# Two hybrid layers on one core: pieces of wide products inside the triangular solves, and a block transpose for a third merge

## The chip, the core and the metric

The kernel runs on one NeuronCore of a Trainium2 chip. Its engines work side by side, each through its own instructions in order: TensorE (PE, matrix products into PSUM), VectorE (DVE, elementwise work, reductions and transposes of 32x32 blocks), ScalarE (ACT, activations and copies), GpSimd (POOL, here memsets, gathers and the issue of some DMAs) and SyncE (SP, issues DMAs). An engine waits at an instruction until what it needs is there, and everything behind it on that engine waits too.

The metric is the device time of one execution in microseconds (us). Before the change it was 4466.47 us, the median of three runs (4464.66 to 4471.57).

## The reference

Two layers work on 256 latent tokens and 256 context tokens of width 1024. Cut to what matters here, a layer is

```python
h = adaLN(RMSNorm(x))
z = h @ w_in                      # r, k, v, decay and rate inputs, conv inputs, gates
# RWKV-7, 16 heads of 64, both directions; per head and token t
S = S * w_t - (S @ kk_t) (kk_t * a_t)^T + v_t k_t^T
y_t = S @ r_t
y_a = (groupnorm(y) + bonus) * sigmoid(g1) @ g2 @ w_oA
y_b = silu(layernorm(depthwise_conv31(u * sigmoid(u2)))) @ w_oB
x += gate1 * ((sigmoid(gA) * y_a + sigmoid(gB) * y_b) @ w_out)
x += gate2 * PEER(adaLN(RMSNorm(x)))   # top-16 of 16384 experts, 8 heads
```

In the last layer the context tokens only feed the recurrent state, so most products there have 256 columns instead of 512. A last RMSNorm gives the output. The change touches only the part called the mixer, from `z` to the inputs of `w_oA`.

## The kernel before

**Chunks and solves.** The recurrence is worked in chunks of 64 tokens. Within a chunk, the tokens' mutual influence is a unit triangular matrix of 64x64 that has to be inverted. The 16 heads go in 8 pairs, one head on the upper and one on the lower 64 partitions. For a pair j, `front(j)` makes what the chunks need: the decay and rate products (`lora`, tile `up`), the key norm (`rnc`, `rnb`), the scaled keys (`KR`, `BK`), then `solve`. `solve` forms the triangular matrices of all 16 (chunk, direction) pairs at once (`pd`, L689, and the off-diagonal blocks `po`, L705). It inverts the 16x16 diagonal blocks on DVE by a recurrence of 15 steps (`Tn`, L715 and L717), then joins blocks by matrix products on PE. A *merge* is 64 matmuls of 32x32 with 32 columns. Three merges (L735, tile `m`) make the inverse of the 32x32 blocks: the first multiplies by `Dg` and is masked into `PA`; the second gives `T32`, the inverse; the third gives `Td`, the transposed inverse, from the transposed factors. Two half merges of 32 matmuls each (L755 and L767, called fourth and fifth here) make the last off-diagonal block. Fp32 matmuls are recorded twice, so a merge has 128 records.

**Chains and wide products.** `chain(j)` then walks through the 8 chunks of pair j with products of 64x64 (tile `p`; `wp` and `tr` beside it), each step waiting for copies on ACT and DVE. `tail(j)` normalises the pair's output. The *wide products* are the columns of `w_in`: `project(j)` makes k, r and v of a pair (24 products), `conv(j)` two products per group of conv channels, `gate(i)` one for each of 16 groups of gates, `lora_g(i)` two. Each is done by `dense_w`: 24 matmuls of 128x128 (tile `dn`, lines L350 to L352) with 512 or 256 columns, three for each of 8 pieces of the weights, which are split into a high and a low part (`whi`, cast on ACT, L132; `wlo`, subtracted on DVE, L133). There are two buffers for each of raw, high and low weights. `conv_sum(j)` does the depthwise convolution on DVE, and `conv_ln`, `yb` (tile `dn` from `chi`) and `gg` (tile `gp`) finish the mixer behind the last pair.

**What sets the order.** Each of these is a Python generator, registered by `job` with a start, an end and a number of steps. The loop at the end of the mixer (L985) always takes one step of the live job whose due time is earliest; times are counted in pairs of heads. A job's first step first runs those it needs to their end. All of `project(2..7)`, `conv`, `gate` and `lora_g` stand in one line (`order`, L949 to L971), each needing the one before it, spread evenly over 0 to `DENSE` = 7.5, and a piece of it is three matmuls. The steps that `solve` yields are weighed (`W_MRG`, `W_SMALL`, `W_TRI`). The compiler's scheduler then places instructions of each engine by priority in about that order, and gives buffers from what is free.

Of the kernel before, what the change touches and what calls it, by code (L numbers as in the profile page):

```python
# [88 lines left out]
def body(ctx: ExitStack, tc: tile.TileContext, I, out):  # L89
# [125 lines left out]
    for l in range(2):  # L215
# [74 lines left out]
        with tc.tile_pool(name="psR", bufs=1, space=PSUM) as pr, tc.tile_pool(name="rw", bufs=1) as rw:  # L290
# [381 lines left out]
            def solve(KR, BK, TT, extra):  # L672
# [11 lines left out]
                for d in range(2):  # L684
                    for c in range(8):
                        for b in range(2):
                            for hh, hs in enumerate(heads):
                                q, cs = hh * 64 + 32 * b, slice(32 * b, 32 * b + 32)
                                mm(pd[q:q + 32, d * 8 + c], BK[d][hs, c // 2, 1 + c % 2, cs], KR[d][hs, c, 0, cs],  # L689
                                   start=True, stop=True)  # L690
                        if c % 2 == 1:
                            yield 0.25
# [9 lines left out]
                for d in range(2):  # L702
                    for c in range(8):
                        for hh, hs in enumerate(heads):
                            mm(po_[lo_[hh], d * 8 + c], BK[d][hs, c // 2, 1 + c % 2, 0:32], KR[d][hs, c, 0, 32:64],  # L705
                               start=True, stop=True)
                        if c % 4 == 3:
                            yield 0.25
# [23 lines left out]
                def merge(pq, lhs, rhs):  # L732
                    for u in range(16):
                        for q in quads:
                            mm(pq[q, u], lhs[q, u], rhs[q, u], start=True, stop=True)  # L735
                        if u % MU == MU - 1:
                            yield W_MRG * MU
# [10 lines left out]
                pq = pt("m3")  # L748
                yield from merge(pq, PA, T16t)
                dve.tensor_tensor(Td, pq, T16t, op=OP.add)  # L750
                yield W_SMALL
                pq = pt("m4")
                for u in range(16):
                    for hh in range(2):
                        mm(pq[hi_[hh], u], Of[lo_[hh], u], T32[lo_[hh], u], start=True, stop=True)  # L755
                    if u % MU == MU - 1:
                        yield W_MRG * MU / 2
# [7 lines left out]
                for u in range(16):  # L765
                    for hh in range(2):
                        mm(pq[lo_[hh], u], PB[hi_[hh], u], Td[hi_[hh], u], start=True, stop=True)  # L767
                    if u % MU == MU - 1:
                        yield W_MRG * MU / 2
# [157 lines left out]
            def step(i):  # L927
                t0, t1, n, gen, needs, k = jobs[i]
                for d in needs if k == 0 else ():
                    while jobs[d][3] is not None:  # L930
                        step(d)
                w = next(gen, jobs)
                if w is jobs:
# [3 lines left out]

            def due(i):
# [3 lines left out]
            NF = 4 * W_LORA + 2 * W_RMS + 15 * W_TRI + 15 * W_VEC + 12 * W_SMALL + 32 * W_MRG * 2 + 3.2  # L942
# [5 lines left out]
            job(conv_sum(0), 0, 0.5, 19, cv0)  # L948
            order = []  # L949
            for j in range(2, 8):  # L950
                order += [("p", j), ("c", j - 1)] + [("g", None)] * (1 if j < 7 else 0)
            order += [("c", 7)] + [("g", None)] * 11 + [("z", 0), ("z", 1)]
            njobs = sum({"p": 3, "c": 2, "g": 1, "z": 1}[a] for a, _ in order)
            t, gi, prev = 0.0, 0, None
            for a, j in order:
                if a == "p":
                    g, n = project(j), 3
                elif a == "c":
                    g, n = conv(j), 2
                elif a == "g":  # L960
                    g, n = gate(gi), 1
                    gi += 1
                else:
                    g, n = lora_g(j), 1
                t1 = t + n * DENSE / njobs
                prev = job(g, t, t1, 8 * n, *([] if prev is None else [prev]))
                if a == "p":
                    pj[j] = prev
                elif a == "c":
                    lastc = job(conv_sum(j), t1, t1 + 0.5, 19, prev)  # L970
                t = t1  # L971
# [540 lines left out]
```

## Time and profile before

| | before |
|---|---|
| median of 3 runs | 4466.47 us |
| profiled execution | 4484.19 us, span of instructions 4482.4 us |
| PE busy | 4079.7 us (91%) |
| DVE busy | 3190.2 us (71%) |
| ACT busy | 2108.8 us (47%) |
| POOL busy | 275.1 us (6%) |
| mean granted clock of TensorE | 0.927 |
| mixer of layer 0 | about 60 to 988 us |
| mixer of layer 1 | about 2640 to 3440 us |

The span runs from the first to the last instruction. Busy PE is not PE at its best: a matmul counts as busy from its start to a modelled end, and at the lower of the two clock levels (1.2 instead of 2.4 GHz) it simply takes longer. The clock granted is a mean over the stretch asked for, where 1.00 is the full level and 0.50 the lower one.

### The profile page before, as it was taken

What the parts mean: (1) busy time and instruction counts of PE and PEld (TensorE: products, weight loads), DVE (VectorE), ACT (ScalarE), POOL (GpSimd) and SP (SyncE); (2) the same over time, 40 slices, a digit from 0 to 9 for tenths busy, and PEclk for the clock granted to TensorE, in tenths of its full rate; (3) what the DMA queues carried; (4) which work ended last, traced back from release to release, by engine and by line L of the source; (5) the groups of instructions that cost most, each with busy time, mean ns of one, the idle gap of its engine ahead of it and who ended that gap; (6) DMA issues with size and microseconds to landing.
All of it is one profiled execution on the core that took longest, in us unless ns stands there. A gap on an engine that the chain in (4) does not pass through costs nothing. (4 is left out here: it accounts for less than half of the span.)

```text
span 4482.4 us, 84925 instructions
## 1 busy us (share of the span) xinstructions
PE 4079.7 (91%) x34103; PEld 3303.5 (74%) x34103; DVE 3190.2 (71%) x6780; ACT 2108.8 (47%) x3810; POOL 275.1 (6%) x323
## 2 busy tenths in 40 slices
PE   8999999998988887899998989899998799899998
PEld 6666677666778887788777867677776678787776
DVE  6777778557898988667776656466555779877665
ACT  5344444423337656333333354444444457785444
POOL 0000000000001111111111000000000000000000
PEclk8899899989999999999999998788987899999999
DMA  4111112256347768987787621111124656669875
GB/s 162 46 52 49 41 49 65 76 176 202 115 146 274 265 230 322 324 284 278 279 290 282 210 73 60 33 42 49 52 67 161 212 186 198 215 222 306 285 249 171
DMA packets 313147, 762.01 MB, mean 170 GB/s; under 512 B 29808, under 2 KB 176816, under 8 KB 293296
## 3 DMA queue, kind: packets, MB, share of 16 engines
q1 hardware_dynamic: 255664, 568.36, 38.3%
q0 software_dynamic: 24448, 151.01, 9.0%
q10 hardware_dynamic: 32640, 37.21, 2.3%
q8 instruction: 268, 4.39, 0.4%
q14 instruction: 127, 1.04, 0.1%
HBM read 665.80 MB, written 90.67 MB: 169 GB/s over the span
## 5 line engine op out<-in xcount | busy, mean ns | idle before, releaser
L132 ACT CAST whi<-wraw 128x1024 fp32r<-128x1024 f32 x456 | 477.5, 1047 | 666.4 <-PE sE L1080 169.7
L133 DVE TENSOR_TENSOR wlo<-wraw,whi 128x1024 fp32r<-128x1024 f32 x456 | 553.7, 1215 | 170.9 <-ACT whi L132 169.4
L1369 PE MATMUL v<-vl,ah 128*128 128x512 f32 x1280 | 408.1, 401 | 52.4 <-DVE vl L133 52.2
L132 ACT CAST vh<-vraw 128x1024 fp32r<-128x1024 f32 x256 | 268.3, 1049 | 331.8 <-PE v L1369 183.8
L1369 PE MATMUL v<-vh,ah 128*128 128x512 f32 x1280 | 404.6, 398 | 12.5 <-ACT vh L132 11.2
L1369 PE MATMUL v<-vh,al 128*128 128x512 f32 x1280 | 404.2, 397 | 12.0 <-DVE al L133 11.8
L1079 PE MATMUL sE<-hl,whi 128*128 128x384 f32 x1024 | 360.2, 352 | 49.6 <-ACT whi L132 36.9
L350 PE MATMUL dn<-hhi,whi 128*128 128x512 f32 (+1 forms) x928 | 383.6, 413 | 10.3 <-DVE v L312 2.8
L1075 PE MATMUL sE<-hl,whi 128*128 128x512 f32 x1024 | 374.4, 406 | 10.8 <-ACT whi L132 10.5
L1081 PE MATMUL sE<-hl,wlo 128*128 128x384 f32 x1024 | 354.7, 348 | 30.7 <-DVE wlo L133 30.6
L352 PE MATMUL dn<-hhi,wlo 128*128 128x512 f32 (+1 forms) x928 | 354.9, 383 | 2.7 <-DVE wlo L133 1.6
L351 PE MATMUL dn<-hlo,whi 128*128 128x512 f32 (+1 forms) x928 | 354.2, 382 | 0.0
L1080 PE MATMUL sE<-hl,whi 128*128 128x384 f32 x1024 | 352.9, 345 | 0.0
L133 DVE TENSOR_TENSOR vl<-vraw,vh 128x1024 fp32r<-128x1024 f32 x256 | 311.9, 1219 | 42.4 <-ACT vh L132 41.7
L1369 PEld LDWEIGHTS v<-vl,ah 128*128 128x128 f32 x1280 | 242.6, 192 | 118.3 <-DVE vl L133 68.1
L1369 PEld LDWEIGHTS v<-vh,al 128*128 128x128 f32 x1280 | 243.4, 191 | 71.7 <-DVE al L133 19.4
L1369 PEld LDWEIGHTS v<-vh,ah 128*128 128x128 f32 x1280 | 244.2, 192 | 65.5 <-ACT vh L132 14.4
L1349 DVE TENSOR_TENSOR gl<-gl,Gt 128x256 f32<-128x256 f32 (+1 forms) x192 | 91.7, 479 | 262.2 <-DMA gl<-Sd 253.1
L1077 PE MATMUL sE<-hl,wlo 128*128 128x256 f32 x896 | 261.3, 292 | 17.1 <-DVE wlo L133 16.1
L1137 POOL DMA_INDIRECT gu<-in_uv,eiG x128 | 189.0, 1477 | 1214.5 <-DVE accG L1162 1010.8
L1079 PEld LDWEIGHTS sE<-hl,whi 128*128 128x128 f32 x1024 | 200.1, 195 | 57.8 <-ACT whi L132 39.4
L1081 PEld LDWEIGHTS sE<-hl,wlo 128*128 128x128 f32 x1024 | 199.6, 195 | 35.5 <-DVE wlo L133 35.1
(383 smaller groups left out, 8820.0 us busy)
## 6 DMA issues: line engine op xcount, KB each, us to landing
wraw<-in_u SPq DMA_DIRECT2D x256, 512.0 KB, 4.0
vraw<-in_v SPq DMA_DIRECT2D x256, 512.0 KB, 4.7
wraw<-in_w_main SPq DMA_DIRECT2D x116, 512.0 KB, 3.5
adaraw<-in_ada_w SPq DMA_DIRECT2D x88, 512.0 KB, 4.9
gd<-Gs SPq DMA_DIRECT2D x20, 2048.0 KB, 11.2
Gt<-gd SPq DMA_DIRECT2D x32, 768.0 KB, 8.3
wraw<-in_w_q SPq DMA_DIRECT2D x32, 512.0 KB, 3.7
Gt<-gd SPq DMA_DIRECT2D x32, 512.0 KB, 5.4
```

The source lines that it names most:

```text
L132: act.copy(hi, src)
L133: dve.tensor_sub(lo, src, f32(hi))
L350: mm(ps[:m, :n], wh(k), xh(k), start=k == 0, stop=False)
L351: mm(ps[:m, :n], wh(k), xl(k), start=False, stop=False)
L352: mm(ps[:m, :n], wl(k), xh(k), start=False, stop=k == KT - 1)
L1075: mm(ps[:, :2 * EN], wh[:, k], hl[:, k].rearrange("p a n -> p (a n)"), start=first, stop=last)
L1077: mm(ps[:, EN:2 * EN], wl[:, k], hl[:, k, 0], start=False, stop=False)
L1079: mm(ps[:, :n], wh[:, k], hl[:, k, 0, :n], start=first, stop=False)
L1080: mm(ps[:, :n], wh[:, k], hl[:, k, 1, :n], start=False, stop=False)
L1081: mm(ps[:, :n], wl[:, k], hl[:, k, 0, :n], start=False, stop=last)
L1137: pool.indirect_dma_start(g, None, I[f"uv{l}"], bass.IndirectOffsetOnAxis(ap=eiG[:, k:k + 1].bitcast(U32), axis=0), bounds_check=NKEY * NK ...
L1369: mm(acc[t][d], a[:, ts], v[:, d * 512:d * 512 + 512], start=first and i == 0, stop=last and i == 2)
```

## The change

It does three things, all in the mixer. First, a function `more()` steps the next job of a list `wide` once, unless that job is being stepped already or needs something that isn't done. `solve` calls it inside its products and merges, so that one piece of a wide product (three matmuls) is issued there, whatever its due time. The fourth and fifth merges yield half as often. Second, the one line of wide products becomes two: `conv`, `gate` and `lora_g` stand in the line that `more` draws from, in a pattern of two gates and one conv, where a conv also needs the sum of the conv before it; each `project(j)` now has due times of its own, one pair ahead of its `front`. Third, the third merge and its add are replaced by one DVE transpose of 32x32 blocks, from `T32` to `Td`. `NF` is the count of steps of a front.

```diff
                 dve.tensor_tensor(T32, pq, T16, op=OP.add)
-                pq = pt("m3")
-                yield from merge(pq, PA, T16t)
-                dve.tensor_tensor(Td, pq, T16t, op=OP.add)
+                more()
+                dve.transpose(Td.rearrange("p c t -> p (c t)"), T32.rearrange("p c t -> p (c t)"))
+                more()
                 yield W_SMALL
...
                         for q in quads:
                             mm(pq[q, u], lhs[q, u], rhs[q, u], start=True, stop=True)
                         if u % MU == MU - 1:
+                            more()
                             yield W_MRG * MU
...
                         mm(pq[hi_[hh], u], Of[lo_[hh], u], T32[lo_[hh], u], start=True, stop=True)
-                    if u % MU == MU - 1:
-                        yield W_MRG * MU / 2
+                    if u % (2 * MU) == 2 * MU - 1:
+                        more()
+                        yield W_MRG * MU
...
+                busy.add(i)
                 w = next(gen, jobs)
+                busy.discard(i)
...
+            wide = []
+            def more():
+                for i, need in wide:
+                    if jobs[i][3] is not None:
+                        if i not in busy and (need is None or jobs[need][3] is None):
+                            step(i)
+                        return
...
+            sums = {0: job(conv_sum(0), 0, 0.5, 19, cv0)}
+            order = [("c", j) for j in range(1, 8)]
+            for i in range(16):
+                order.insert(i + i // 2, ("g", i))
+            order += [("z", 0), ("z", 1)]
...
+                last = job({"c": conv, "g": gate, "z": lora_g}[a](j), t, t1, 8 * w,
+                           *([] if last is None else [last]), *([sums[j - 1]] if a == "c" else []))
+                wide.append((last, sums[j - 1] if a == "c" else None))
...
-                if a == "p":
-                    pj[j] = prev
+                pj[j] = job(project(j), FRONT * (j - 2) + 0.1, FRONT * (j - 1) - 0.1, 24, pj[j - 1])
```

By count, 1024 matmul instructions (16 solves of 64) and 16 adds go and 16 transposes come; everything else is issued as often as before, in another order. Three places show it.

PE in layer 1, solve 4, from the first merge on; before (`m` with `Dg` is the first merge, with `PA,T16t` the second, with `T16t,PA` the third, with `Of` the fourth):

```order
L735 MATMUL m_29170<-T_29164,Dg 32x32 x64
L351 MATMUL dn<-hlo,whi 128x512
L352 MATMUL dn<-hhi,wlo 128x512
L350 MATMUL dn<-hhi,whi 128x512
L351 MATMUL dn<-hlo,whi 128x512
L735 MATMUL m_29270<-PA,T16t 32x32 x64
L735 MATMUL m_29367<-T16t,PA 32x32 x64
L755 MATMUL m_29455<-T_29254,Of 32x32 x32
```

Three merges and a half merge stood there with four wide matmuls among them. The same place now:

```order
L737 MATMUL m_28483<-T_28477,Dg 32x32 x64
L891 MATMUL p_28419<-KR,S 64x64 x2
L893 MATMUL p_28419<-WT_23756,VS_23748 64x64 x2
L891 MATMUL p_28419<-KR,S 64x64 x2
L893 MATMUL p_28419<-WT_23756,VS_23748 64x64 x2
L350 MATMUL dn<-hhi,whi 128x256
L351 MATMUL dn<-hlo,whi 128x256
L352 MATMUL dn<-hhi,wlo 128x256
L737 MATMUL m_28588<-PA,T16t 32x32 x32
L350 MATMUL dn<-hhi,whi 128x256
L351 MATMUL dn<-hlo,whi 128x256
L352 MATMUL dn<-hhi,wlo 128x256
```

The second merge is cut into pieces with wide matmuls between them, and so it goes on to the fifth.

PE in layer 0, solve 7 (the last), from the first merge on; before:

```order
L735 MATMUL m_9098<-T_9092,Dg 32x32 x32
L350 MATMUL dn<-hhi,whi 128x512
L351 MATMUL dn<-hlo,whi 128x512
L352 MATMUL dn<-hhi,wlo 128x512
L735 MATMUL m_9098<-T_9092,Dg 32x32 x32
L799 MATMUL wp<-KR,BK 128x128 x2
L849 MATMUL p_9179<-VS_379,WT_383 64x64 x2
L852 MATMUL p_9179<-S,KR 64x64 x2
```

And now, in the same place:

```order
L737 MATMUL m_8696<-T_8683,Dg 32x32 x64
L857 MATMUL p_8808<-S,KR 64x64
L351 MATMUL dn<-hlo,whi 128x512
L352 MATMUL dn<-hhi,wlo 128x512
L865 MATMUL p_8808<-B,TT_367 64x64 x4
L350 MATMUL dn<-hhi,whi 128x512
L737 MATMUL m_8788<-PA,T16t 32x32 x64
L877 MATMUL p_8808<-VS_379,BV 64x64 x4
L351 MATMUL dn<-hlo,whi 128x512
L352 MATMUL dn<-hhi,wlo 128x512
L804 MATMUL wp<-KR,BK 128x128 x2
L758 MATMUL m_8906<-T_8783,Of 32x32 x32
```

Here the pieces between the merges have become fewer: what could be drawn was waiting for a convolution's sum, or used up.

PE in layer 1, where one wide product ends and the next starts, with the tiles' numbers; before, at solve 6:

```order
L350 MATMUL dn_25592<-hhi_24185,whi_25588 128x512
L351 MATMUL dn_25592<-hlo_24186,whi_25588 128x512
L352 MATMUL dn_25592<-hhi_24185,wlo_25589 128x512
L350 MATMUL dn_25688<-hhi_24185,whi_25684 128x256
L735 MATMUL m1_24861<-T16_24851,Dg_24686 32x32 x64
L351 MATMUL dn_25688<-hlo_24186,whi_25684 128x256
```

And now, at solve 2:

```order
L352 MATMUL dn_26354<-hhi_23665,wlo_26351 128x256
L350 MATMUL dn_26278<-hhi_23665,whi_26274 128x512
L737 MATMUL m2_26475<-PA_26370,T16t_26359 32x32 x48
L351 MATMUL dn_26278<-hlo_23666,whi_26274 128x512
L352 MATMUL dn_26278<-hhi_23665,wlo_26275 128x512
L737 MATMUL m2_26475<-PA_26370,T16t_26359 32x32 x16
L350 MATMUL dn_26570<-hhi_23665,whi_26566 128x256
L351 MATMUL dn_26570<-hlo_23666,whi_26566 128x256
L352 MATMUL dn_26570<-hhi_23665,wlo_26567 128x256
```

Before, one product followed the other. Now `dn_26278` (a projection) is open while `dn_26354` ends and `dn_26570` starts, so both buffers of split weights are taken until `dn_26354` is through.

## Rows read from the trace of the kernel before

**Rows 1.** Windows: us; PE, PEld, DVE, ACT, POOL busy (instructions); clock; DMA share, GB/s

```profile
173.00:812.00 639.00, 629.89 (x8958) 446.35 (x8947) 469.48 (x1174) 272.60 (x548) 23.45 (x62) 0.96 0.16 50
812.00:893.00 81.00, 77.98 (x596) 52.33 (x594) 46.60 (x89) 40.78 (x76) 1.63 (x3) 0.96 0.26 84
...
2685.00:3322.00 637.00, 581.62 (x9578) 450.77 (x9578) 385.41 (x1015) 297.73 (x584) 26.73 (x57) 0.85 0.16 50
3322.00:3380.00 58.00, 53.42 (x506) 41.94 (x506) 32.24 (x80) 35.05 (x72) 1.98 (x3) 0.88 0.26 78
```

**Rows 2.** Waits of PE, layer 1, 2685 to 3322: us, times, longest

```profile
PE m L735 <- issue: 22.3, 13, 3.0
PE m L755 <- issue: 6.7, 5, 2.5
...
PE dn L352 <- DVE wlo L133: 0.9, 2, 0.7
```

**Rows 3.** Windows of layer 1's solves 0 to 7, merges and 15 us behind

```profile
2717.80:2748.30 30.50, 26.41 (x602) 21.68 (x602) 8.47 (x15) 11.66 (x20) 1.20 (x2) 0.66 0.13 41
2800.20:2829.70 29.50, 26.08 (x627) 20.04 (x626) 8.45 (x18) 13.34 (x23) 1.18 (x2) 0.71 0.09 25
2879.30:2911.80 32.50, 27.02 (x645) 21.07 (x645) 9.43 (x24) 13.42 (x25) 1.19 (x2) 0.74 0.08 23
2968.00:3000.60 32.60, 28.68 (x640) 21.40 (x641) 7.22 (x16) 12.13 (x22) 1.22 (x2) 0.76 0.08 23
3050.80:3084.90 34.10, 28.34 (x603) 20.64 (x603) 7.50 (x16) 10.21 (x20) 1.22 (x2) 0.60 0.10 35
3139.80:3173.60 33.80, 33.33 (x707) 24.58 (x708) 15.09 (x35) 15.09 (x31) 1.23 (x2) 1.00 0.12 38
3217.80:3251.10 33.30, 30.74 (x667) 23.95 (x667) 11.21 (x30) 13.76 (x30) 0.54 (x1) 0.69 0.12 41
3304.40:3336.90 32.50, 27.54 (x649) 23.04 (x649) 8.25 (x16) 10.47 (x23) 0.00 (x0) 0.68 0.14 42
```

**Rows 4.** The like windows of layer 0's solves 2 and 4

```profile
308.30:344.90 36.60, 36.60 (x708) 25.09 (x709) 24.32 (x58) 15.88 (x31) 1.94 (x5) 1.00 0.16 49
...
498.80:540.00 41.20, 39.68 (x666) 26.28 (x666) 22.62 (x49) 13.68 (x29) 1.94 (x5) 0.71 0.15 48
```

**Rows 5.** Groups, layer 1: the third merge; busy us, mean ns, idle before

```profile
L735 PE MATMUL m<-T16t,PA 32*32 32x32 f32 x1024 | 14.8, 211 | 16.4 <-issue 16.4
```

**Rows 6.** Timeline of PE, layer 0: start us, us, instruction

```profile
307.81 0.39 PE L351 MATMUL dn<-hlo,whi 128*128 128x512 f32 x1
308.04 0.40 PE L352 MATMUL dn<-hhi,wlo 128*128 128x512 f32 x1
308.37 0.75 PE L735 MATMUL m<-T,Dg 32*32 32x32 f32 x64
309.05 0.50 PE L350 MATMUL dn<-hhi,whi 128*128 128x512 f32 x1
309.39 0.40 PE L351 MATMUL dn<-hlo,whi 128*128 128x512 f32 x1
```

**Rows 7.** Groups, layer 0: the third merge

```profile
L735 PE MATMUL m<-T16t,PA 32*32 32x32 f32 x1024 | 13.5, 197 | 4.2 <-issue 4.2
```

**Rows 8.** Timeline of PE behind the mixer of layer 0

```profile
993.57 0.63 PE L152 MATMUL ya<-olo,whi 128*128 128x512 f32 x1
994.00 0.63 PE L153 MATMUL ya<-ohi,wlo 128*128 128x512 f32 x1
```

**Rows 9.** Groups, layer 1, 2685 to 3322: split weights, transpose, add

```profile
L133 DVE TENSOR_TENSOR wlo<-wraw,whi 128x1024 fp32r<-128x1024 f32 x47 | 57.2, 1217 | 5.3 <-ACT whi L132 4.8 <-issue 0.4
L132 ACT CAST whi<-wraw 128x1024 fp32r<-128x1024 f32 x47 | 49.2, 1047 | 29.3 <-PE dn L351 25.9 <-DVE Tn L717 3.2
...
L728 DVE STREAM_TRANSPOSE T16t<-Ty 128x512 f32<-128x512 f32 x8 | 8.4, 1045 | 0.0
...
L750 DVE TENSOR_TENSOR Td<-m,T16t 128x512 f32<-128x512 f32 x8 | 5.5, 691 | 23.3 <-PE m L735 23.3
```

More of the change, by code (lines that the diff above doesn't have):

```diff
@@ L747, in solve @@
                 dve.tensor_tensor(T32, pq, T16, op=OP.add)
-                pq = pt("m3")
-                yield from merge(pq, PA, T16t)
-                dve.tensor_tensor(Td, pq, T16t, op=OP.add)
+                more()
+                dve.transpose(Td.rearrange("p c t -> p (c t)"), T32.rearrange("p c t -> p (c t)"))
+                more()
                 yield W_SMALL
@@ L755, in solve @@
                         mm(pq[hi_[hh], u], Of[lo_[hh], u], T32[lo_[hh], u], start=True, stop=True)
-                    if u % MU == MU - 1:
-                        yield W_MRG * MU / 2
+                    if u % (2 * MU) == 2 * MU - 1:
+                        more()
+                        yield W_MRG * MU
                 for x in hi_:
@@ L767, in solve @@
                         mm(pq[lo_[hh], u], PB[hi_[hh], u], Td[hi_[hh], u], start=True, stop=True)
-                    if u % MU == MU - 1:
-                        yield W_MRG * MU / 2
+                    if u % (2 * MU) == 2 * MU - 1:
+                        more()
+                        yield W_MRG * MU
                 for x in lo_:
@@ L936, in step @@
                     jobs[i][5] = k + (w or 1)
+            wide = []
[5 more added lines that the diff above has]
+                        return
+            busy = set()
             def due(i):
@@ L940, in due @@
                 return t0 + (t1 - t0) * min(1.0, k / n)
-            NF = 4 * W_LORA + 2 * W_RMS + 15 * W_TRI + 15 * W_VEC + 12 * W_SMALL + 32 * W_MRG * 2 + 3.2
+            NF = 4 * W_LORA + 2 * W_RMS + 15 * W_TRI + 15 * W_VEC + 20 * W_SMALL + 32 * W_MRG * 2 + 3.2
             pj, fj, cj = {}, {}, {}
@@ L947, in body @@
             cv0 = job(conv(0), -LEAD * 0.4, 0, 16)
-            job(conv_sum(0), 0, 0.5, 19, cv0)
-            order = []
-            for j in range(2, 8):
[L951 to L955, printed above, removed]
-                if a == "p":
[L957 to L967, printed above, removed]
-                    pj[j] = prev
-                elif a == "c":
-                    lastc = job(conv_sum(j), t1, t1 + 0.5, 19, prev)
-                t = t1
+            sums = {0: job(conv_sum(0), 0, 0.5, 19, cv0)}
[3 more added lines that the diff above has]
+            order += [("z", 0), ("z", 1)]
+            n = sum({"c": 2, "g": 1, "z": 1}[a] for a, _ in order)
+            t, last = 0.0, None
+            for a, j in order:
+                w = 2 if a == "c" else 1
+                t1 = t + w * DENSE / n
+                last = job({"c": conv, "g": gate, "z": lora_g}[a](j), t, t1, 8 * w,
+                           *([] if last is None else [last]), *([sums[j - 1]] if a == "c" else []))
+                wide.append((last, sums[j - 1] if a == "c" else None))
+                if a == "c":
+                    lastc = sums[j] = job(conv_sum(j), t1, t1 + 0.5, 19, last)
+                t = t1
+            prev = last
+            for j in range(2, 8):
+                pj[j] = job(project(j), FRONT * (j - 2) + 0.1, FRONT * (j - 1) - 0.1, 24, pj[j - 1])
             for j in range(1, 8):
```

## The prediction

> **What bounds the kernel now.** Read first where the engines stand by stage, with the granted clock of TensorE beside them. Only the two mixers change in the order of instructions; what lies between and behind them (988 to 2640 us and from 3440 us) is issued in the same order as before. Four stretches matter [rows 1]. In layer 0 (512 columns per wide product), while the eight solves run, PE is busy 629.9 of 639 us at a clock of 0.96: PE itself is the bound there. In layer 1 (256 columns in most products) the same stretch takes 637 us, but PE is busy only 581.6, and its clock is 0.85. A clock of c is a mix of two levels, so a share 2(1-c) of the time runs at the lower one (1.2 GHz): 0.30 of 637, about 191 us. DVE is busy 385 of 637, ACT 298: neither is full. So layer 1 loses time in two ways: 55.4 us of idle PE and a halved clock.
>
> Next, what PE waits for in layer 1 [rows 2]: 22.3 + 6.7 = 29.0 of the 55.4 us stand on the merges (L735, L755) with the releaser "issue": PE waited for nothing that the profile shows, in 18 pieces of up to 3 us, inside long unbroken runs of 32x32 matmuls. Then the clock, solve by solve: one window from the first merge to 15 us behind the last one [rows 3]. Seven of eight have a clock of 0.60 to 0.76 and PE idle for 2.6 to 5.8 us; the sixth (solve 5) has 1.00 and 0.5 us idle. By the order of instructions solve 5 has 33 wide matmuls between its merges, the others 4 to 22. In layer 0, where 24 to 32 lie there from solve 1 on, the like window of solve 2 has 1.00, but that of solve 4 only 0.71 [rows 4]. Wide matmuls between the merges go with a full clock mostly, not always.
>
> **The change, part by part.**
>
> *The third merge goes.* It is 64 matmuls a solve (two records each), 512 a layer. In layer 1 its group is busy 14.8 us, with 16.4 us idle before it, all "issue" [rows 5]: 31.2 us, on PE's path, since the other engines are not full. In layer 0 PE is packed, so the start-to-start time counts: 64 records from 308.37 to 309.05, 0.68 us [rows 6], times 16 is 10.9, and 4.2 us idle before it [rows 7]: 15.1 us. The least that this saves is the time in which PE works on it, 14.8 + 10.9 = 25.7 us, if every stall comes back in the second merge; the most is 46.3, which I take: in the new order a piece of wide product stands where most stalls were.
>
> *Edges of wide runs.* Two wide matmuls start 0.23 us apart; from a wide one to a merge it is 0.33 (308.04 to 308.37), and the first wide one behind a merge takes 0.34 (309.05 to 309.39) [rows 6]. A run of wide matmuls thus costs 0.10 + 0.11 = 0.21 us of edges. By the two orders there are 358 such runs in layer 0 before and 341 after, 293 and 284 in layer 1: -3.6 and -1.9 us, though layer 1's merges themselves fall into 53 pieces instead of 44. The Trainium skill (TensorEngine Tiling (Array Packing), Key Properties) says that a change of tiling mode drains the engine, which speaks against cutting merges into small pieces. By that rule, with a whole 0.40 us matmul run out at each edge, 26 runs fewer would be 20.8 us and each further piece of a merge 0.8 us; the rows show a quarter of it, and the sum goes by the rows.
>
> *Other stalls in layer 1's merges.* 29.0 - 16.4 = 12.6 us. In the new order solves 2, 3, 4 and 6 have 27 to 33 wide matmuls in the stretch (4, 6, 8 and 11 before); solves 0, 1 and 7 stay nearly bare (20, 9, 15). Four of seven bare ones: 7.2 us; ends 0 and 12.6.
>
> *The clock in layer 1.* Two wide matmuls at the lower clock start 0.43 us apart (993.57 to 994.00) [rows 8] against 0.23: of time at the lower clock 1 - 0.23/0.43 = 0.47 is lost. Window length times (1-c) over the seven bare windows [rows 3] is 69.6, so 69.6 x 2 x 0.47 = 65 us are lost in them; over solves 2, 3, 4 and 6 it is 40.2, or 38 us. Ends: 0 and 65. Since a window with 33 wide matmuls kept the clock and one with 25 in layer 0 did not, I take half of 38: 19 us.
>
> *The transpose.* One DVE transpose (1.05 us) stands where an add (0.69) stood [rows 9]: 0.36 us times 16 is 6 us of DVE. Only the copy into TT and the fifth merge read its result; the fourth merge with its wide pieces and two ACT copies cover it. I take 0; bare it is +6, and DVE no longer waits 23.3 us for the third merge ([rows 9], idle before Td).
>
> *Two wide products open at once.* Before, all wide products form one line; now projections and the rest are two. By the orders, products that start while another is open go from 3 to 33 in layer 0 and from 8 to 27 in layer 1: 49 more. There are two buffers for split weights, so such a product can be split only when one of the open ones ends: cast 1.05 us, then subtraction 1.22 [rows 9], 2.26 us, with PE's next wide matmul queued behind. In the order 5 to 30 rows of other PE work stand in that gap, often one merge. Ends: 0, and 49 x 2.26 = 111 us if every one is exposed. The nearest row is the wait for wlo in layer 1 now: 0.9 us [rows 2] over 8 such starts, 0.11 each; 49 times that is 5.5. I take +6, 3 a layer. The weight loads on SP, the stores of gates on ACT's and of convolutions on POOL's queue are as many as before and move with their pieces.
>
> *Work taken from the ends.* What fills the solves is missing behind the last one: 150 wide matmuls stood there in layer 0 and 78 do now, 126 and 39 in layer 1. That is 72 x 0.23 = 16.6 us and, at half the columns, 87 x 0.115 = 10.0 us more before, and as much less behind, if PE sets the pace there. It nearly does in layer 0 (78.0 of 81 us busy), less in layer 1 (53.4 of 58) [rows 1], and the chains of the last heads then stand alone. In layer 0 the last convolution also moves behind the last solve, some 17 us of DVE, which has 34 us free there. Ends: 0 and +26.6. I take half, +8 and +5.
>
> *Layer 0's bare solve.* Solve 7 has 5 wide matmuls in its stretch, 27 before. At layer 1's price for a bare one (65/7 of clock and 12.6/7 of stalls) that is +11. Solve 4 goes from 25 to 45; its window lost 41.2 x 0.29 x 2 x 0.47 = 11.2 us [rows 4], of which I take half back: net +5.5, ends -11 and +11.
>
> *Sum.* Layer 1: -31.2 - 1.9 - 7.2 - 19 + 3 + 5 = -51.3. Layer 0: -15.1 - 3.6 + 3 + 8 + 5.5 = -2.2. Together -53.5 against the profiled execution of 4484.19 us (span 4482.4 and 1.8 around it): 4430.7. That execution is 17.7 us above the median of the runs, 4466.47; the difference taken off the median gives **4413 us**.
>
> **The rivals.**
>
> *A second merge as bare as the third (4451).* The clock does not come back: the pieces drawn in layer 1 are mostly 256 columns, and the first merge still runs as one block of 64. For it: the layer 0 window at 0.71 with 25 wide matmuls. Against: solve 5 at 1.00. Without the 19, with the full +26.6 at the ends and +11 for the bare solve: -46.3 - 5.5 - 7.2 + 6 + 26.6 + 11 = -15.4. In this case the drawn pieces don't do what they are put in for.
>
> *Idle, not small tiles, lowers the clock (4345).* All seven windows that fell have PE idle for 2.6 us or more, the one that did not 0.5 [rows 3]; with the third merge and the stalls gone, the three bare ones recover too. Against: layer 0's 0.71 with 1.5 us idle. Then 65 and 12.6 us come back in layer 1, no solve 7 dip in layer 0: -46.3 - 5.5 - 12.6 - 65 - 11 + 6 + 13 = -121. The Trainium skill (TensorE: Matmul & The Clock Gate, What's actually happening) has it so: the throttled state is the default and recent busyness of the engine releases it.
>
> *The split weights come late (4518).* PE takes its instructions in order, so a wide matmul whose weights wait for a free buffer stops the chain and the solve behind it. At 2.26 us for each of 49 more starts the sum turns to -53.5 - 6 + 111 = +51, slower. It breaks even where 26 of the 49 are exposed in full (59.5/2.26). For: the shortest gaps, 5 rows. Against: those rows hold 1 to 2 us of work, raw weights are loaded ahead in any case, and 8 such starts now cost 0.9 us.
>
> **How the numbers follow.** Chances: forecast 0.52, bare merges 0.22, idle rule 0.16, late weights 0.10 (partly exposed in most of it, so that 0.03 of it is no change). The forecast's own range is 4390 to 4436 (half the clock term and the ends, 9.5 + 13, either way). The range of 4350 to 4459 goes from near the idle rival, half of which it leaves out, to no visible gain, and leaves out most of the late-weights case. Of a kernel of this length 0.2% (9 us) is about what can be told from no change. The forecast, the idle rival and three quarters of the bare one lie below 4457.5: 0.84 faster. A quarter of the bare case and 0.03 make 0.09 within, the remaining 0.07 is slower.
>
> **What would show it.** Right: layer 1's stretch from the first pd to the last fifth merge near 590 us, with issue waits on merges under 8 us, and a clock above 0.9 in the windows of solves 2, 3, 4 and 6; layer 0's stretch about as long as now, with a dip at solve 7. The clock term is wrong if those windows stay near 0.7; the buffer term if PE's waits for whi and wlo go above 10 us; the end term if the time from the last fifth merge to the last gp in either layer doesn't shrink at all. A longer solve stretch in layer 1 would overturn the whole account.

## The result and the profile after

The changed kernel takes 4392.82 us, the median of four runs (4383.36 to 4406.58). The kernel before, beside it, took 4465.96. The ratio is 0.9836, with an interval of 0.9806 to 0.9866. The forecast was 4413 in a range of 4350 to 4459, and faster. The profiled execution, the slowest of the four, took 4406.58 us (span 4404.8).

First the stages, as in [rows 1] but each from its first to its last event: solves of layer 0, what stands behind them up to `ya`, and the same of layer 1. Profile after; columns: stretch, length, then the busy time of PE, PEld, DVE, ACT and POOL, the granted clock, DMA share, GB/s:

```profile
100.70:810.80 710.10, 696.64 (x9008) 496.07 (x9007) 517.09 (x1283) 323.38 (x621) 25.51 (x67) 0.95 0.16 52
810.80:977.00 166.20, 156.67 (x1001) 104.98 (x1000) 113.91 (x223) 65.70 (x121) 7.01 (x13) 0.85 0.40 131
2657.00:3262.10 605.10, 572.18 (x8598) 441.36 (x8598) 393.06 (x1012) 311.16 (x598) 25.44 (x55) 0.89 0.17 54
3262.10:3395.20 133.10, 110.01 (x865) 86.70 (x864) 70.52 (x172) 50.47 (x109) 6.89 (x12) 0.74 0.36 118
```

The same four stretches of the kernel before, in a second profile of it (4476.06 us, the run f4_before below):

```profile
99.50:817.40 717.90, 701.53 (x9967) 496.41 (x9968) 526.90 (x1305) 302.00 (x603) 26.03 (x68) 0.94 0.15 49
817.40:1000.10 182.70, 174.07 (x1068) 118.80 (x1067) 107.30 (x200) 72.71 (x129) 6.50 (x12) 0.88 0.39 128
2672.70:3321.80 649.10, 594.70 (x9578) 458.85 (x9577) 385.72 (x1015) 297.75 (x583) 26.73 (x57) 0.83 0.15 49
3321.80:3461.30 139.50, 121.47 (x934) 98.17 (x933) 73.60 (x172) 59.59 (x121) 6.86 (x12) 0.77 0.38 124
```

In the first profile of before they were 709.2, 183.0, 636.9 and 141.3 us. Layer 1's solves are 32 to 44 us shorter, layer 0's 8 us at most; the end of layer 0 is 17 us shorter, that of layer 1 six to eight. Two profiles of one kernel thus differ by up to 12 us in a stretch, so below I read stretches as a guide and leave verdicts to the timed ratios.

PE's waits in layer 1, which answer to [rows 2] (engine, tile, line, releaser: us, times, longest):

```profile
PE m L737 <- issue: 5.5, 7, 1.6
PE dn L352 <- DVE wlo L133: 1.7, 4, 0.5
...
PE m L758 <- issue: 1.1, 2, 0.7
```

Of 29.0 us of "issue" on the merges, 6.6 are left; what PE waits for there no run shows. The windows of layer 1's solves 0 to 7, which answer to [rows 3]:

```profile
2688.30:2714.30 26.00, 23.93 (x472) 17.73 (x474) 8.40 (x18) 12.91 (x22) 1.21 (x2) 0.69 0.12 41
2767.00:2793.80 26.80, 25.20 (x527) 18.84 (x527) 10.75 (x31) 14.99 (x29) 2.39 (x4) 0.94 0.15 48
2839.70:2868.60 28.90, 28.68 (x578) 21.44 (x579) 14.38 (x38) 16.91 (x32) 1.78 (x3) 1.00 0.14 48
2914.00:2945.10 31.10, 29.51 (x524) 20.46 (x523) 12.29 (x27) 13.43 (x26) 1.78 (x3) 0.76 0.14 45
3005.10:3037.00 31.90, 31.25 (x601) 23.22 (x600) 14.80 (x36) 15.77 (x33) 2.55 (x5) 1.00 0.14 44
3083.80:3113.80 30.00, 28.02 (x577) 21.65 (x576) 15.27 (x37) 16.62 (x33) 2.98 (x5) 1.00 0.16 50
3158.30:3191.10 32.80, 32.36 (x564) 24.75 (x565) 14.59 (x34) 16.72 (x33) 0.56 (x1) 0.82 0.12 39
3245.50:3277.10 31.60, 27.45 (x579) 22.38 (x578) 11.88 (x30) 12.70 (x31) 0.56 (x1) 0.75 0.22 69
```

Four of eight windows now stand at 0.94 or more, before it was one. So far this looks as forecast: the pieces of wide products went between the merges, the stalls shrank and the clock came back. The experiments say otherwise.

### The profile page after: what moved, and what is told of

Its sections match the earlier page's. It is cut to its first block, busy times and chain, and to the rows that moved or that the text cites. A ratio compares the mean times of both kernels' runs of the same rounds, so it can differ in the third digit from the quotient of the medians.

```text
span 4404.8 us, 80879 instructions
## 1 busy us (share of the span) xinstructions
PE 4034.4 (92%) x32055; PEld 3268.2 (74%) x32055; DVE 3194.0 (73%) x6780; ACT 2131.3 (48%) x3826; POOL 277.7 (6%) x323
## 5 line engine op out<-in xcount | busy, mean ns | idle before, releaser
L1093 PE MATMUL sE<-hl,whi 128*128 128x384 f32 x1024 | 357.3, 349 | 45.8 <-ACT whi L132 34.6
L1383 PEld LDWEIGHTS v<-vl,ah 128*128 128x128 f32 x1280 | 243.2, 192 | 117.1 <-DVE vl L133 66.9
L1383 PEld LDWEIGHTS v<-vh,al 128*128 128x128 f32 x1280 | 244.1, 192 | 65.8 <-DVE al L133 13.1
L1093 PEld LDWEIGHTS sE<-hl,whi 128*128 128x128 f32 x1024 | 197.9, 193 | 53.5 <-ACT whi L132 37.2
```

The lines of the kernel that those rows point to most:

```text
L1093: mm(ps[:, :n], wh[:, k], hl[:, k, 0, :n], start=first, stop=False)
L1383: mm(acc[t][d], a[:, ts], v[:, d * 512:d * 512 + 512], start=first and i == 0, stop=last and i == 2)
```

## The experiments

Times are medians, each ratio against the kernel before run beside it: 4462.95 us for the runs whose names start with e, 4463.09 for f, 4468.86 for g. Comparisons between two groups go by these ratios and are weaker than those within one.

### Which of the three parts gains

My theory was that the drawing brings the clock and the stalls, the transpose the third merge's own 46 us. The rival: one part does it all.

**e1_transpose**: the kernel before with the third merge replaced, nothing else (its `NF` gets the 16 steps fewer).

```diff
-                pq = pt("m3")
-                yield from merge(pq, PA, T16t)
-                dve.tensor_tensor(Td, pq, T16t, op=OP.add)
+                dve.transpose(Td.rearrange("p c t -> p (c t)"), T32.rearrange("p c t -> p (c t)"))
```

> The kernel before with only the third merge turned into the block transpose (no pieces drawn, one line of wide products; NF less by that merge's steps). My account: the merge is worth its busy time and the stalls before it, 31 us in layer 1 and 15 in layer 0, so 4466 - 46 = about 4420, of which at most 10 us is lost again to a second merge that now stalls; the clock in layer 1's merge windows stays at 0.6 to 0.76 where the merges stay bare (solves 2 to 7). Rival (stalls move to the second and fourth merge): only the busy time goes, 26 us, about 4440, with issue waits on merges in layer 1 still near 29 us.

Measured 4395.38, ratio 0.9833 (0.98 to 0.9866): all of the gain, and more than either expected value. The windows that I expected to stay at 0.6 to 0.76 didn't all do so either: solves 3, 4 and 7 of layer 1 have 1.00.

**e2_draw**: the changed kernel with the three lines of the third merge put back in the place of the transpose and its two `more()`.

> The changed kernel with the third merge and its add kept (pieces are drawn in that merge too). My account: what is left is drawing and the two lines, clock and stalls in layer 1: 4393 + 26 (busy time of the third merge) = about 4420 to 4430, issue waits on merges in layer 1 under 10 us, clock above 0.9 in the windows of solves 2 to 6 there. Rival (the transpose is the whole gain): 4455 to 4466.

Measured 4465.09, ratio 1.001 (0.9987 to 1.0032): no gain. But the windows that I had named did recover, with the third merge still there. Layer 1's solves 2, 3, 4 and 6:

```profile
2878.70:2912.00 33.30, 33.21 (x720) 24.32 (x722) 15.95 (x39) 17.16 (x33) 2.24 (x4) 0.96 0.19 62
2962.10:2997.00 34.90, 34.50 (x733) 25.69 (x733) 15.98 (x41) 15.99 (x31) 1.78 (x3) 1.00 0.19 59
3041.70:3078.10 36.40, 35.36 (x663) 26.05 (x662) 13.74 (x28) 13.88 (x27) 1.78 (x3) 0.67 0.18 57
3220.60:3251.50 30.90, 30.90 (x699) 24.38 (x698) 15.70 (x35) 16.75 (x33) 0.56 (x1) 0.94 0.19 62
```

Before they had 0.74, 0.76, 0.60 and 0.69 [rows 3]. Yet layer 1's solves as a whole take 646.4 us at 0.85, before 636.9 at 0.85 and 649.1 at 0.83: what came back in these windows was lost elsewhere in the stretch.

**e3_lines**: as e2_draw, and `more()` draws nothing, so only the two lines of wide products and the changed step weights are left.

```diff
-                for i, need in wide:
+                for i, need in ():
```

> As e2_draw but the drawing does nothing: only the two lines of wide products (projections on their own due times) and the steps' weights of the changed kernel. By the order of instructions 10 to 25 wide matmuls now stand in layer 1's merges even so, and 78 and 49 behind the last solve instead of 150 and 126. My account has the gain with the drawn pieces: 4445 to 4460, issue waits between 10 and 29 us. Rival (the second line does it, not the drawing): the same time as e2_draw within 9 us.

Measured 4489.3, ratio 1.0048 (1.0021 to 1.0075), above both expected values. The two lines cost about half a per cent, and drawing gives that back.

**e4_again**: the changed kernel once more.

> The changed kernel once more, unchanged, for the spread of its time and of its stages: 4383 to 4407. My account of the mixers (about 56 us shorter in the first pair of profiles) holds if the two mixers again take 55 to 60 us less than in the profile of before, while the stages with the same order of instructions (from the mixer of layer 0 to that of layer 1, and behind the latter), 10 us shorter each in the first pair, move to either side by up to 10 us. Rival (the change also shortens those stages): they are 20 us shorter again.

Measured 4402.65, ratio 0.9866 (0.9836 to 0.9895). By the timed runs of this group the rival of e2_draw holds: the transpose alone is the gain, and my division of it was wrong. The second profile of the changed kernel, the four stretches, then layer 1's solves 3 and 6:

```profile
100.60:798.50 697.90, 684.45 (x9008) 487.97 (x9007) 516.92 (x1283) 322.88 (x621) 25.51 (x67) 0.97 0.17 53
798.50:963.90 165.40, 153.36 (x1000) 103.23 (x1001) 113.78 (x223) 65.58 (x121) 7.01 (x13) 0.88 0.42 132
2651.00:3245.60 594.60, 560.49 (x8598) 434.11 (x8598) 393.00 (x1012) 310.95 (x598) 25.48 (x55) 0.91 0.18 55
3245.60:3380.70 135.10, 112.50 (x866) 88.91 (x864) 70.63 (x172) 50.41 (x109) 6.90 (x12) 0.73 0.36 116
...
2907.10:2938.30 31.20, 29.61 (x558) 21.68 (x559) 13.58 (x33) 15.26 (x29) 1.78 (x3) 0.92 0.14 45
3144.50:3174.50 30.00, 29.85 (x578) 22.58 (x578) 14.57 (x34) 17.01 (x33) 0.56 (x1) 0.96 0.13 42
```

The mixers together are 77 and 96 us shorter than in the two profiles of before, where I expected 55 to 60; the stretch between them, 1680.0 us in the first profile of the changed kernel, takes 1687.1 here, between the 1692.0 and 1672.6 of before, so the change doesn't shorten that one. It is the same program, yet solve 3 has 0.92 for 0.76 in the first profile and solve 6 0.96 for 0.82.

### Does drawing gain anything once the third merge is gone

**f1_lines_tr**: the changed kernel with the edit of e3_lines (two lines, transpose, no drawing).

> The changed kernel, with the transpose and with two lines of wide products, but more() draws nothing: what is left in the solves comes from due times alone (in order 15, 30, 7, 6, 21, 23, 21, 3 wide matmuls between the merges in layer 0, 93 behind the last solve). With the third merge kept, two lines without drawing were 0.5% slower than before (ratio 1.0048), and drawing gave that back (1.001). Theory A, the lines cost and the drawing repays it, whether the third merge is there or not: about 0.4% above the changed kernel, some 4415 to 4425 us, with the L0 solves again over 710 us. Theory B, the lines only hurt because a third merge stood bare beside them: as fast as the transpose alone, 4390 to 4400. Theory C, drawing is what makes the transpose pay: above 4440, near no gain (against it: the transpose alone gave 0.9833).

Measured 4409.07, ratio 0.9872 (0.9844 to 0.9901), between theories A and B; C is out. Its interval overlaps both of the changed kernel's (0.9836 and 0.9866), so that drawing's part, 0.1 to 0.4 per cent by these ratios, can't be told from nothing.

**f2_line_merge**: e1_transpose, with `more()` at the yields of the two merges left and the one line of before, from which `more` draws (the code for that, as in the change, is left out here; a conv also needs the sum of the conv before it).

```diff
                         if u % MU == MU - 1:
+                            more()
                             yield W_MRG * MU
```

> The transpose, the one line of wide products as it was before, and drawing from that line at the merges alone (not at pd, po, the transpose or the halves): 10, 27, 26, 24, 26, 21, 16, 24 wide matmuls between the merges in layer 0, 19, 17, 9, 14, 16, 25, 9, 19 in layer 1, 150 and 110 behind the last solve. Theory A, drawing gains on its own when nothing else is moved: layer 1's issue waits below the 10 us and its clock above the 0.86 that the transpose alone has, time 4375 to 4390. Theory B, what is drawn in one place is missing in another and PE's time is the same: 4390 to 4400, within 0.3% of the transpose alone, with a clock that differs by solve and not in sum.

Measured 4400.81, ratio 0.9858 (0.9828 to 0.9888): as the transpose alone, theory B.

**f3_line_all**: the same one line, with `more()` at every place of the changed kernel but the second one at the transpose.

> As the one before, but drawing at all the places where the changed kernel draws, from one line of wide products: 40, 10, 33, 33, 36, 31, 33, 23 between the merges in layer 0, 17, 16, 14, 18, 21, 25, 19, 22 in layer 1, 144 and 94 behind the last solve. So no two lines open at once, and no last solve with 5. Theory A, the changed kernel lost its drawing gain to the two lines: here it shows, 4370 to 4385. Theory B, drawing moves work and gains nothing: 4390 to 4400 as the transpose alone. Theory C, drawing itself costs, because it pulls wide matmuls ahead of the solve's own chain: above 4405, L0's solve stretch longer than the 684 us of the transpose alone.

Measured 4434.49, ratio 0.9949 (0.9916 to 0.9983): theory C, drawing everywhere from the one line costs about 1% (0.8% against f2_line_merge, 1.2% against e1_transpose by the ratios). That it does so by pulling wide matmuls ahead of the solve's chain, as theory C has it, isn't shown. Solves of layer 0, then of layer 1, in its profile:

```profile
100.60:806.40 705.80, 686.33 (x8946) 485.78 (x8945) 528.11 (x1306) 307.56 (x608) 26.09 (x68) 0.95 0.16 50
...
2676.10:3298.90 622.80, 585.82 (x8592) 452.24 (x8591) 388.76 (x1018) 296.20 (x585) 26.67 (x57) 0.85 0.16 52
```

Its solves of layer 1 have 14 to 25 wide matmuls between the merges, those of e1_transpose 6 to 30, and the clock is 0.85 here, 0.86 there: more wide work between the small tiles did not raise it.

**f4_before**: the kernel before, for a second profile.

> The kernel before, unchanged, for one more profile of it: how far the stages differ between two profiles of one kernel. If what lies outside the mixers differs by 10 to 20 us between profiles of any kernel (1617 to 1637 us between the mixers in the five so far), this one will differ from the first by as much there, and the two solve stretches (709 and 637 us) should come back within some 15 us. If instead the first profile was an outlier in the solves, they come out nearer 690 and 620, and the gain of the transpose read from stages is smaller than 60 us.

4476.06 us; its stages are shown above. The stretch between the second row and the third was 1672.6 us, against 1692.0 in the first profile, so some 20 us between two profiles lie outside the mixers. Its windows of layer 1's solves 0 to 7, again the stretches of [rows 3]:

```profile
2705.60:2738.10 32.50, 27.70 (x617) 22.63 (x617) 9.89 (x21) 12.49 (x23) 1.21 (x2) 0.68 0.13 39
2800.60:2831.20 30.60, 27.08 (x633) 20.93 (x633) 8.72 (x20) 13.75 (x24) 1.18 (x2) 0.72 0.07 24
2880.40:2913.10 32.70, 28.66 (x647) 22.53 (x647) 9.83 (x26) 13.80 (x27) 1.18 (x2) 0.69 0.08 23
2969.70:3001.90 32.20, 28.32 (x639) 21.16 (x640) 7.19 (x16) 12.09 (x22) 1.22 (x2) 0.76 0.07 24
3052.20:3086.20 34.00, 28.80 (x605) 20.87 (x604) 7.67 (x17) 10.42 (x21) 1.22 (x2) 0.60 0.11 35
3141.00:3174.70 33.70, 33.23 (x708) 24.50 (x708) 14.99 (x34) 15.12 (x31) 1.23 (x2) 1.00 0.12 38
3219.00:3252.00 33.00, 30.55 (x680) 23.60 (x679) 11.36 (x30) 13.81 (x30) 0.54 (x1) 0.74 0.13 42
3305.10:3336.80 31.70, 26.62 (x641) 22.27 (x642) 7.51 (x15) 10.33 (x21) 0.00 (x0) 0.68 0.13 41
```

Solve by solve the clock is within 0.05 of the first profile's, so these dips are not chance alone. But it doesn't always come back: solve 4 of layer 0 has 0.71 in the first profile [rows 4] and 0.63 in this one, and the two profiles of the changed kernel differ by up to 0.16 in layer 1 (0.76 and 0.92 above). What makes a dip is another question.

### Why a merge of 1.4 us costs 4 us

By [rows 6] a merge of 128 records takes 2 x 0.68 = 1.36 us at full clock, 10.9 for the eight of a layer and 21.8 for both. The gain is 68 us (4462.95 - 4395.38), on average some 4 for each of 16 merges. The next four runs ask what in the merge costs that. All start from the base g0_order, where the solve yields the third merge's steps without its work, so that the kernel issues the rest in the order of before. The last three add work whose result nothing reads. On PE, after the compiler's scheduler, the order stays nearly the same in layer 0, but not in layer 1: between the merges of solves 0 to 7 there g0_order has 33, 23, 9, 6, 11, 16, 14 and 8 wide matmuls, g2_unused 25, 7, 10, 16, 20, 33, 13 and 10, the kernel before 22, 8, 4, 6, 8, 33, 11 and 6. So in layer 1 these runs differ in the merge and in an order.

**g0_order**

```diff
-                pq = pt("m3")
-                yield from merge(pq, PA, T16t)
-                dve.tensor_tensor(Td, pq, T16t, op=OP.add)
+                for _ in range(16 // MU):
+                    yield W_MRG * MU
+                dve.transpose(Td.rearrange("p c t -> p (c t)"), T32.rearrange("p c t -> p (c t)"))
```

> The kernel before with the transpose in the place of the third merge, and the solve still yielding the steps of the third merge, so that the order of everything else stays that of before. It is the base for the next three, and a second measurement of the transpose alone (ratio 0.9833 there). If the transpose's gain does not hang on a lucky order: 4390 to 4405. If it does: anywhere up to 4430.

Measured 4374.36, ratio 0.9768 (0.9714 to 0.9823), below the expected window.

**g1_filler**, in front of these yields:

```diff
+                pq = pt("m3")
+                mm(pq.rearrange("p c t -> p (c t)")[:, 0:384], T16t[:, 0:4].rearrange("p c t -> p (c t)"),
+                   PA.rearrange("p c t -> p (c t)")[:, 0:384], start=True, stop=True)
```

> The base, and one matmul of a whole 128x128 tile with 384 columns in fp32 (T16t, PA) where the third merge stood; nothing reads its result. It waits for the same inputs as the third merge and takes PE about as long as the merge's 0.68 us at full clock (estimate: 16 times 0.64 to 0.85, that is 10 to 14 us in all). Theory A, the third merge cost its own time and beyond it stalls and clock that only its small tiles bring: the filler costs 10 to 14 us over the base, 4405 to 4415. Theory B, any PE work at this place, on the solve's chain, costs what the merge costs: 50 us or more over the base, near 4450.

Measured 4418.35, ratio 0.9867 (0.9811 to 0.9924): 44 us over the base, between the two theories. (The 0.68 us in what I expected is half a merge. The filler takes about 0.9 us of PE a solve, so it is to be held against the half merge below.)

**g2_unused**, in the place of these yields:

```diff
+                pq = pt("m3")
+                yield from merge(pq, PA, T16t)
```

> The third merge still runs on PE, but Td comes from the transpose and nothing reads the merge's result: the merge's work without the wait of DVE for it. Theory A, PE's work is what costs: as slow as before, 4455 to 4470. Theory B, what cost was the wait behind it (DVE's 23.3 us for the third merge in layer 1, and what is queued behind that add): near the base, 4395 to 4410.

Measured 4460.51, ratio 0.999 (0.9957 to 1.0023). Theory A: what costs is PE's work with what it brings along; that DVE no longer waits for the merge gains nothing that can be told.

**g3_half**, in the place of these yields:

```diff
+                pq = pt("m3")
+                for u in range(16):
+                    for q in quads if u % 2 else ():
+                        mm(pq[q, u], PA[q, u], T16t[q, u], start=True, stop=True)
+                    if u % MU == MU - 1:
+                        yield W_MRG * MU
```

> As the run before with half of the third merge (32 of its 64 matmuls, every second block; its result is not read). Theory A, cost in proportion to the 32x32 matmuls, as for busy time: half way, 4425 to 4435. Theory C, the stalls (pieces of up to 3 us) and the lower clock come only once a run of small tiles is long enough: 32 matmuls cost clearly less than half of what 64 do, below 4420; or the second half is what is nearly free, above 4445.

Measured 4443.56, ratio 0.9942 (0.9912 to 0.9972). Half of the merge costs 69 of the 86 us that the whole costs. It isn't proportional; the number lies a little under theory C's second window.

The profiles say where. Solves of layer 0 and of layer 1 in g0_order:

```profile
100.00:782.40 682.40, 664.76 (x8941) 471.60 (x8940) 527.39 (x1305) 301.51 (x602) 26.04 (x68) 0.98 0.16 51
...
2648.10:3224.20 576.10, 541.33 (x8557) 419.47 (x8556) 386.39 (x1015) 300.02 (x587) 26.69 (x57) 0.91 0.18 55
```

In g1_filler:

```profile
99.50:787.00 687.50, 672.54 (x8957) 476.62 (x8958) 525.77 (x1305) 304.45 (x604) 26.04 (x68) 0.98 0.16 51
...
2644.50:3244.00 599.50, 565.30 (x8576) 432.99 (x8575) 387.75 (x1016) 298.43 (x588) 26.68 (x57) 0.89 0.17 53
```

In g2_unused:

```profile
100.10:803.60 703.50, 687.90 (x9966) 488.33 (x9966) 526.86 (x1305) 302.52 (x602) 26.06 (x68) 0.96 0.16 50
...
2649.00:3295.10 646.10, 597.49 (x9582) 461.77 (x9581) 387.61 (x1016) 298.82 (x588) 26.77 (x57) 0.84 0.15 50
```

In g3_half:

```profile
100.00:800.30 700.30, 682.01 (x9453) 481.87 (x9454) 526.88 (x1305) 304.39 (x604) 26.05 (x68) 0.96 0.15 50
...
2666.80:3315.80 649.00, 603.76 (x9065) 463.02 (x9064) 387.29 (x1015) 295.31 (x584) 26.70 (x57) 0.82 0.15 49
```

In e1_transpose, the same work in another order:

```profile
100.00:783.60 683.60, 668.96 (x8941) 474.70 (x8942) 526.47 (x1305) 297.88 (x600) 26.01 (x68) 0.98 0.16 51
...
2642.60:3247.60 605.00, 568.26 (x8563) 440.30 (x8562) 385.95 (x1017) 299.79 (x587) 26.70 (x57) 0.86 0.17 52
```

From each pair of rows the difference to g0_order can be split in three. Idle PE is length less busy time. The clock's part is estimated at the prediction's rate, busy time x (1-c) x 0.94, uncertain by some 3 us in each row, since c has two digits. What is left is PE's work at full clock. For g2_unused in layer 1: idle 48.6 - 34.8 = 13.8; clock 89.9 - 45.8 = 44.1; of 70.0 there remain 12.1.

| more than g0_order, us | idle | clock | work | sum |
|---|---|---|---|---|
| layer 0: g1_filler | -2.7 | 0.1 | 7.7 | 5.1 |
| layer 0: g3_half | 0.7 | 13.1 | 4.1 | 17.9 |
| layer 0: g2_unused | -2.0 | 13.4 | 9.8 | 21.1 |
| layer 0: before, mean of two profiles | -1.2 | 23.6 | 8.8 | 31.2 |
| layer 1: g1_filler | -0.6 | 12.7 | 11.3 | 23.4 |
| layer 1: g3_half | 10.5 | 56.4 | 6.0 | 72.9 |
| layer 1: g2_unused | 13.8 | 44.1 | 12.1 | 70.0 |
| layer 1: before, mean of two profiles | 20.1 | 42.7 | 4.1 | 66.9 |
| layer 0: e1_transpose, no third merge | -3.0 | 0.1 | 4.1 | 1.2 |
| layer 1: e1_transpose, no third merge | 2.0 | 29.0 | -2.1 | 28.9 |

For g2_unused the work column comes out at 9.8 and 12.1, where [rows 6] give 10.9 a layer. The added groups in layer 1 (busy us, mean ns, idle before), in g1_filler:

```profile
L749 PE MATMUL m<-PA,T16t 128*128 128x384 f32 x16 | 7.2, 531 | 0.0
```

in g2_unused:

```profile
L735 PE MATMUL m<-T16t,PA 32*32 32x32 f32 x1024 | 13.8, 201 | 16.2 <-issue 16.2
```

and in g3_half:

```profile
L751 PE MATMUL m<-T16t,PA 32*32 32x32 f32 x512 | 8.2, 199 | 6.3 <-issue 6.3
```

So the third merge's price, by g2_unused over both layers, is 22 us of work, 12 of idle PE and 57 of clock, 91 in the profiles (86 in the timed runs): the clock is nearly two thirds. That is against g0_order. The last two rows of the table have no third merge either, and in layer 1 another order alone makes 29 us of clock (two profiles of one program differ by up to 12 us in a stretch). Against e1_transpose the price of the same merge is 61 us: 20 of work, 13 idle, 28 of clock, a little under half. How much of layer 1's clock is the merge's and how much an order's isn't settled.

The "issue" stalls come back with the merge in layer 1, 16.2 us, as 16.4 in [rows 5], and 6.3 with half of it. The clock falls about as far for half a merge as for a whole one; the profiled execution of g3_half lies 17 us above its median and that of g2_unused 10 below, so the rows make the half look a little dearer than it is.

In layer 0, where PE hardly waits and the order is nearly the same, a 128x128 matmul in the same place costs its own time and no clock, half a merge of about the same busy time 13 us of clock. The filler takes the merge's PSUM buffer too, so in layer 0 the buffer alone isn't the cost. But the dip is not one of every merge: some 10 of the whole merge's 13 us in layer 0 are lost in solve 0, and the windows of the other seven stand at 1.00 with the merge as without it. Solve 0 in g0_order, then in g2_unused:

```profile
127.80:153.80 26.00, 24.77 (x504) 17.66 (x505) 21.20 (x51) 14.00 (x26) 1.41 (x3) 1.00 0.16 48
...
128.50:158.30 29.80, 27.30 (x571) 18.63 (x572) 17.89 (x37) 11.25 (x18) 1.18 (x2) 0.64 0.15 42
```

In layer 1 the filler costs clock too, and 13.2 us more at the end behind the solves (152.4 against 139.2 us, the last row of the four stages of each), which I can't explain.

## Why the prediction was right, and where it was not

The time and the sign came out, the division didn't.

**The third merge.** I took 46.3 us for its own time and stalls, with 25.7 as the least; the table gives 34 (22 + 12). The failed step came with it: in the prediction no clock came back with the third merge itself; all 19 us of the clock term hung on the pieces drawn. By the table it was 57 us with the merge, 28 against the order of e1_transpose. The transpose alone gains 68 (e1_transpose) to 94 us (g0_order); drawing and two lines together gain nothing measurable (1.001 with the third merge, without it f1_lines_tr against the changed kernel and f2_line_merge against e1_transpose). The merge's work and stalls were taken too high, its clock at nothing, and a clock gain was booked on the drawing: that this adds up to -53.5, against -60 (e4_again) and -73, was luck.

**The clock in layer 1.** The windows of solves 2, 3, 4 and 6 stand at 1.00, 0.76, 1.00 and 0.82: two of the four above 0.9. In e4_again it is 1.00, 0.92, 1.00 and 0.96, all four, as forecast. The sign came, and it doesn't show what I took it for. By the prediction's rate (an estimate) these windows lost 38 us before and 14 in e2_draw, 24 back for the 19 that I took; but the time of e2_draw is that of before, and layer 1's solves as a whole have no better a clock there. And with the transpose alone, and 6 to 8 wide matmuls between the merges, e1_transpose has full clock in solves 3 and 4, and 0.60 in solve 1 with 23. Its windows of solves 1 and 3:

```profile
2755.90:2786.20 30.30, 29.13 (x505) 21.86 (x503) 9.75 (x20) 14.09 (x23) 1.18 (x2) 0.60 0.18 58
...
2925.60:2953.40 27.80, 25.72 (x575) 19.69 (x575) 10.00 (x28) 15.79 (x29) 1.20 (x2) 1.00 0.08 28
```

These rows also speak against the rival of idle PE: 1.2 us idle at 0.60, 2.1 us idle at 1.00. The Trainium skill (TensorE: Matmul & The Clock Gate, What's actually happening) has recent busyness release the clock; in these two windows the busier one is the slower. Neither count decides a window. What does is open. Shown is only this: of solve stretches with and without the third merge, in what order the compiler then makes, those without it have the better clock (layer 0 and 1: 0.98 and 0.91 in g0_order, 0.96 and 0.84 in g2_unused; 0.95 and 0.89 in the changed kernel, 0.94 and 0.85 in e2_draw). One stretch goes the other way, layer 0 of f1_lines_tr with 0.93 against 0.95 in e3_lines.

**Stalls.** 6.6 us are left on the merges, forecast under 8. But without any drawing 9.2 are left in e1_transpose and 6.9 in g0_order, so the term of 7.2 comes with the transpose too; with drawing and the third merge 16.0 are left in e2_draw.

**Two products open at once.** Waits for `wlo` are 1.7 us in layer 1, taken 3; the rival of late weights, worth 111 us, didn't happen. The two lines do cost: 1.0048 in e3_lines. The solves of layer 0 take 733.0 us in its profile, 709.2 and 717.9 in those of before, while its end is only 9 us shorter (173.4). I had looked for this cost in the buffers only.

**The ends.** Layer 0's end shrank by the full 16.6 us, of which I took half; layer 1's by four to eight of 10.0 over the two profiles of either kernel.

**Layer 0's bare solve.** No dip: the window of solve 7 has 1.00 with 5 wide matmuls.

```profile
699.40:737.90 38.50, 38.50 (x558) 25.31 (x557) 18.91 (x45) 12.59 (x25) 0.00 (x0) 0.79 0.09 30
798.70:825.80 27.10, 26.56 (x582) 18.99 (x580) 21.23 (x55) 10.81 (x25) 0.00 (x0) 1.00 0.12 36
```

The dip in this profile stands at solve 6 (the first row, 0.79), with 43 wide matmuls between its merges; in e4_again that window has 0.96. With the third merge and 5 wide ones solve 7 does dip: 0.66 in e2_draw.

Layer 0 as a whole, solves and end, went from 892 and 901 us (two profiles) to 876 and 863, that is by 16 to 37 us and not by the -2.2 of the sum; layer 1 by 40 to 59, where the sum has 51.3. Layer 1's solves were to come near 590 us: 605.1 and 594.6.

**The transpose** at nothing: `Td` takes 0.71 us and has no wait.

```profile
L752 DVE STREAM_TRANSPOSE Td<-T 128x512 f32<-128x512 f32 x8 | 5.7, 710 | 0.1
```

The best version is g0_order, 4374.36 us: before's order with the transpose. Its ratio of 0.9768 (0.9714 to 0.9823) lies below e4_again's interval and overlaps that of the first timing slightly; the two were not timed side by side. It differs from e1_transpose only in the steps that the solve yields and their count, so its lead over that run may be the luck of an order.

## What to carry to other kernels

A block of small-tile matmuls can cost several times its busy time: price it by the time and the granted clock of the whole stretch around it, not of the windows alone, and in more than one order, since another order of the same work moved layer 1's solves by 29 us between two profiles. Here half of the block gave back little. When a change bundles a removal with a reordering, run the removal alone first; here the reordering had a plausible story in the profile and no measurable part in the gain. An agreeing total doesn't confirm its terms.

## What the runs showed of the hardware

The transpose of 32x32 blocks within one contiguous tile took 0.71 us, about the add it replaced (0.69), where the strided one took 1.05 [rows 9]. The clock of a window came back within 0.05 in a second profile of the kernel before in all eight windows of layer 1, but moved by 0.16 and 0.14 in two of the changed kernel's. And the same eight matmuls of 128x384 cost 5.1 us in layer 0's solves and 23.4 in layer 1's, where the order of the rest moved with them.
